# Every second 2 MB load of the experts' weights issued by ScalarE instead of SyncE

## The chip, the cores and the metric

The kernel runs on one core of one Trainium2 chip. The metric is the device time of one execution in microseconds; a time quoted for a kernel is the median of its runs, and the profile is of one execution.

## The reference

A two-layer decoder trunk for 256 tokens of width 1024, all in float32. Layer 0: chunkwise retention (4 heads) and a dense SwiGLU (width 2816). Layer 1: sparse attention with compressed, selected and window branches, and then the part that the change touches, a mixture of 8 SwiGLU experts of width 3584, of which each token uses two:

```python
logits = xf @ w_router
top_v, top_i = lax.top_k(logits, 2)
w = softmax(top_v)
gate = sum(one_hot(top_i, 8) * w[..., None], axis=1)
for e in range(8):
    out = out + gate[:, e:e + 1] * swiglu(xf, w_in[e], w_out[e])   # (256,1024)@(1024,7168), (256,3584)@(3584,1024)
```

Each block ends with a layer norm of `alpha * x + f(x)`. The experts' weights are 352 MB of the 444 MB that the kernel reads.

## The kernel before, in words

The program is a list of steps (`step`), emitted in an order written out by hand; each engine runs its own instructions in exactly that order. A step names the weight units that it reads. The driver at the end of `tile_decoder` goes through the list: it converts units ahead of need (`convert`, L238: ScalarE makes the rounded high part `whi`, VectorE the rest `wlo`; in the experts nothing is converted), emits the step, and releases the units that it has read (`release`, L225). When a whole slot is released, `release` calls `load_next`, which emits the next load of the list into the slot that came free. So a load's place in the program is just behind the last reader of its slot, and the engine that issues it waits there for that reader.

Weights come into SBUF in one list of loads. Those of the layers before the experts are 1 MB each (`z.wide` is None, L208). Those of the experts are 2 MB each, 128 partitions by 16 KB (L204, `Slot` with `wide`): `units_m` (L1212) makes 14 for an expert's `w_in` and 7 for its `w_out`, 21 for each of 8 experts, and they are loaded in the order in which they are read. Eight slots of 2 MB hold them: four in `ring` (shared with the earlier layers), one `more` (opened in `moe_open`, L1357, where attention's memory is free) and three `ext` (opened in `moe_more`, L1364, on the memory of `whi` and `wlo`). All these loads are issued by SyncE, into one queue.

An expert has four stages s = 0 to 3 (two 128-column chunks of width per column group, the last stage one): `w_in(e, s)` multiplies the gathered tokens `xg` with four slots (two in stage 3), 32 tokens in each of three groups; the third group is behind a branch on the expert's token count (more than 64 tokens). ScalarE applies SiLU, VectorE multiplies (L1262, L1263), `h_transpose` (L1271) turns the result with PE and copies it to `hT` with ScalarE and VectorE, and `w_out(e, s)` (L1290, matmuls on L1301) follows one `w_in` later. `scatter` adds the expert's result to `X3`. All 256 tokens fit the first pass here, so `overflow` does no trip.

The first eight loads are emitted before the first expert's steps are through. Counted from 0: loads 0 and 1 among the q projections (released by conversions of the output weights' first units, just ahead of `att_scores(0, 0)`), load 2 in the last steps of attention, load 3 in `moe_open`, ahead of the last conversion, loads 4, 5 and 6 in `moe_more`, ahead of `moe_ln0` (layer norm, whose square root on ScalarE, L311, comes with a load of ScalarE's function table), and load 7 behind the first slot of expert 0 (its ring slot had been free long before). In the layer norm, VectorE's L314 is followed by the reciprocal of that root (L315) and the scaling (L322).

Of the kernel before, what the change touches and what calls it, by code (L numbers as in the profile page):

```python
# [33 lines left out]
NRAW = 8  # L34
# [73 lines left out]
def tile_decoder(ctx, tc, x, ret_w_in, ret_gn_g, ret_w_out, nsa_w_kv, cmp_k_pe, cmp_k_w1, cmp_k_w2,  # L108
                 cmp_v_pe, cmp_v_w1, cmp_v_w2, nsa_w_q, nsa_w_out, ffn_w_in, ffn_w_out,
                 moe_router, moe_w_in, moe_w_out, ln_g, ln_b, tab_c, tab_r, out, wst, stop=None, cap=CAP):  # L110
    nc = tc.nc
# [76 lines left out]
        return r  # L188

    ring = sb.tile([128, NRAW * 2048], F32, name="ring")  # L190
    state = {"at": 0, "free": NRAW, "loaded": 0, "conv": 0, "raw": [], "more": [], "ext": []}

    def load(z):
        n = len(z.raws)
        if z.kind == "more":
            ap = ptile([128, n * 2048], F32, "more", bufs=NMORE, lv=0)
        elif z.kind == "ext":
            ap = side["pool"].tile([128, n * 2048], F32, name="ext", tag="ext", bufs=NEXT)
        else:
            i = (state["at"] + z.room - n) % NRAW  # L200
            state["at"] += z.room
            ap = ring[:, i * 2048:(i + n) * 2048]
        if z.wide is not None:
            nc.sync.dma_start(ap, z.wide() if callable(z.wide) else z.wide)  # L204
        for i, r in enumerate(z.raws):
            r.ap = ap[:, i * 2048:(i + 1) * 2048]
            for view, src in r.parts:
                nc.sync.dma_start(view(r.ap), src)  # L208

    def load_next(kind="raw"):  # L210
        i = state["loaded"]
        if i < len(order) and not (kind != "raw" and order[i].last):
            if kind == "raw":
                n = len(order[i].raws)
                order[i].room = n + state["at"] % n
                if state["free"] < order[i].room:
                    return False
                state["free"] -= order[i].room
            state["loaded"] += 1
            order[i].kind = kind  # L220
            state[kind].append(order[i])
            load(order[i])
            return kind == "raw"
# [185 lines left out]
    def ptile(shape, dt, tag, bufs=1, lv=-1):  # L409
        return phases[lv][1].tile(shape, dt, name=tag, tag=tag, bufs=bufs)  # L410
# [1227 lines left out]
```

## Time and profile before

| | us |
|---|---|
| median of 3 runs (lowest to highest) | 1444.34 (1441.13 to 1444.92) |
| profiled execution: time, span | 1444.41, 1442.5 |
| PE busy | 1354.2 (94%) |
| VectorE (DVE) busy | 471.3 (33%) |
| ScalarE (ACT) busy | 346.8 (24%) |
| DMA, whole span | 450.78 MB, 313 GB/s |

PE is the matrix engine, DVE is VectorE, ACT is ScalarE, SP is SyncE, POOL is GpSimd; a q behind a name (SPq, ACTq) is the engine's sequencer, which waits and issues DMAs without being counted as busy. L204 is line 204 of the kernel. In a timeline row stand the start and the duration in us, the engine, the line, the operation, what is written and read, the shapes and the count of merged instructions, and in brackets the engine's idle time before it with what ended it. The profiled execution is within the runs shown.

### The profile page before, as it was taken

How to read it: one execution, taken by the hardware profiler on the slowest of the kernel's cores; microseconds unless marked ns; L12 is line 12 of the kernel's file. 1: busy time of each engine (PE TensorE's matmuls, PEld its weight loads, DVE VectorE, ACT ScalarE, POOL GpSimd, SP SyncE). 2: the span in 40 equal slices, each digit the busy share in tenths (PEclk: the TensorE clock that was granted, in tenths of full speed). 3: DMA queues.
4: the chain of work that ended last, by engine and by line, in shares of the span. 5: the costliest groups of instructions: out<-in, count | busy, mean ns of one | idle time of the engine just before them, and what ended most of it. 6: DMA issues, size and time to landing. Idle time of an engine off the chain costs nothing. (4 is left out here: it accounts for less than half of the span.)

```text
span 1442.5 us, 25322 instructions
## 1 busy us (share of the span) xinstructions
PE 1354.2 (94%) x11073; PEld 777.8 (54%) x11073; DVE 471.3 (33%) x845; ACT 346.8 (24%) x653; POOL 62.7 (4%) x74
## 2 busy tenths in 40 slices
PE   8999999999999898899999999989999998879995
PEld 7888878999977657534334333333333343223341
DVE  5756776455574886100100100101001101001002
ACT  4433434444544563200100101011001010000002
POOL 3101101000011100200000000000000000000000
PEclk9999999999999999799999999999999999999997
DMA  9736444555444305899999999999999999999960
GB/s 386 270 137 228 152 186 145 198 203 192 176 152 149 144 1 214 330 426 424 426 426 425 426 425 424 426 424 426 426 426 426 426 425 426 425 425 426 425 269 33
DMA packets 39829, 450.78 MB, mean 313 GB/s; under 512 B 4544, under 2 KB 4704, under 8 KB 7952
## 3 DMA queue, kind: packets, MB, share of 16 engines
q1 hardware_dynamic: 38016, 443.76, 75.1%
q0 software_dynamic: 1536, 4.98, 1.0%
q8 instruction: 108, 1.77, 0.5%
q14 instruction: 25, 0.20, 0.0%
q10 hardware_dynamic: 144, 0.07, 0.0%
HBM read 447.74 MB, written 1.05 MB: 311 GB/s over the span
## 5 line engine op out<-in xcount | busy, mean ns | idle before, releaser
L1239 PE MATMUL mm<-ring,xg 128*32 128x512 f32 (+1 forms) x2336 | 235.8, 554 | 9.9 <-DMA ring<-w_moe_a_dram 5.9
L1263 DVE TENSOR_TENSOR msh<-msh,mm 128x256 f32<-128x256 f32 (+1 forms) x96 | 35.4, 386 | 501.2 <-ACT msh L1262 501.2
L248 DVE TENSOR_TENSOR wlo<-ring,whi 128x1024 fp32r<-128x1024 f32 (+2 forms) x162 | 187.7, 1208 | 32.4 <-ACT whi L247 32.1
L1239 PE MATMUL mm<-ext,xg 128*32 128x512 f32 (+1 forms) x1888 | 182.8, 536 | 6.0 <-DMA ext<-w_moe_a_dram 3.0
L1239 PEld LDWEIGHTS mm<-ring,xg 128*32 128x32 f32 x2336 | 77.7, 111 | 157.9 <-issue 133.6
L247 ACT CAST whi<-ring 128x1024 fp32r<-128x1024 f32 (+2 forms) x162 | 153.7, 1008 | 18.9 <-PE acc L257 12.2
L1262 ACT ACTIVATE msh<-mm 128x256 f32<-128x256 f32 (+1 forms) x96 | 32.2, 356 | 485.4 <-PE mm L1239 485.4
L381 PE MATMUL mm<-xTh,whi 128*128 128x256 f32 x448 | 126.7, 283 | 1.6 <-ACT whi L247 1.6
L1239 PEld LDWEIGHTS mm<-ext,xg 128*32 128x32 f32 x1888 | 66.3, 111 | 114.7 <-issue 93.9
L383 PE MATMUL mm<-xTh,wlo 128*128 128x256 f32 x448 | 126.3, 282 | 0.8 <-DVE wlo L248 0.8
L1301 PE MATMUL acc<-ring,hT 128*32 128x512 f32 x1040 | 119.2, 600 | 7.5 <-DMA ring<-w_moe_o_dram 6.5
L382 PE MATMUL mm<-xTl,whi 128*128 128x256 f32 x448 | 126.1, 281 | 0.0
L1301 PE MATMUL acc<-ext,hT 128*32 128x512 f32 x848 | 94.9, 593 | 4.5 <-DMA ext<-w_moe_o_dram 4.2
L381 PEld LDWEIGHTS mm<-xTh,whi 128*128 128x128 f32 x448 | 84.9, 189 | 2.9 <-ACT whi L247 1.9
L383 PEld LDWEIGHTS mm<-xTh,wlo 128*128 128x128 f32 x448 | 85.0, 190 | 1.0 <-DVE wlo L248 1.0
L382 PEld LDWEIGHTS mm<-xTl,whi 128*128 128x128 f32 x448 | 85.0, 190 | 0.8
L1286 DVE COPY hT<-mm 128x256 f32<-128x256 f32 (+1 forms) x32 | 12.4, 389 | 215.7 <-PE mm L1279 215.7
L1301 PEld LDWEIGHTS acc<-ring,hT 128*32 128x32 f32 x1040 | 36.8, 111 | 82.2 <-issue 70.1
L1284 ACT COPY hT<-acc 128x512 f32<-128x512 f32 (+1 forms) x32 | 17.1, 535 | 223.1 <-PE acc L1279 146.9
L1239 PE MATMUL mm<-more,xg 128*32 128x512 f32 (+1 forms) x640 | 63.2, 541 | 3.8 <-DMA more<-w_moe_a_dram 2.5
L1301 PEld LDWEIGHTS acc<-ext,hT 128*32 128x32 f32 x848 | 29.2, 110 | 65.5 <-issue 56.2
L255 PE MATMUL mm<-whi,xTh 128*128 128x512 f32 (+1 forms) x144 | 55.7, 387 | 0.3 <-ACT xTh L260 0.2
(325 smaller groups left out, 1669.7 us busy)
## 6 DMA issues: line engine op xcount, KB each, us to landing
ring<-w_moe_a_dram SPq DMA_DIRECT2D x55, 2048.0 KB, 27.2
ext<-w_moe_a_dram SPq DMA_DIRECT2D x42, 2048.0 KB, 27.7
ring<-w_moe_o_dram SPq DMA_DIRECT2D x29, 2048.0 KB, 27.7
ext<-w_moe_o_dram SPq DMA_DIRECT2D x21, 2048.0 KB, 27.2
more<-w_moe_a_dram SPq DMA_DIRECT2D x15, 2048.0 KB, 28.5
ring<-w_ffn_b_dram SPq DMA_DIRECT2D x22, 1024.0 KB, 5.8
ring<-w_ret_a_dram SPq DMA_DIRECT2D x16, 1024.0 KB, 8.6
more<-w_moe_o_dram SPq DMA_DIRECT2D x6, 2048.0 KB, 26.5
```

Source lines behind the costliest of these rows:

```text
L247: nc.scalar.copy(u.hi, v)
L248: nc.vector.tensor_sub(u.lo, v, u.hi.bitcast(F32))
L255: nc.tensor.matmul(ps, xh, wh, start=start, stop=False, skip_group_check=True)
L381: nc.tensor.matmul(ps, u.hi[:, k], xh[:, k], start=start and k == 0, stop=False, skip_group_check=True)
L382: nc.tensor.matmul(ps, u.hi[:, k], xl[:, k], start=False, stop=False, skip_group_check=True)
L383: nc.tensor.matmul(ps, u.lo[:, k], xh[:, k], start=False, stop=k == KD - 1, skip_group_check=True)
L1239: nc.tensor.matmul(M["A", g][j * 32:(j + 1) * 32, :n], M["xg", e // 2][:, k, e % 2, g * 32:(g + 1) * 32], v[:, kk, j], start=k == 0, stop= ...
L1262: nc.scalar.activation(sh[:, g, :w], M["A", g][:, :w], AF.Silu)
L1263: nc.vector.tensor_mul(sh[:, g, :w], sh[:, g, :w], M["A", g][:, w:2 * w])
L1284: nc.scalar.copy(dst, src)
L1286: nc.vector.tensor_copy(dst, src)
L1301: nc.tensor.matmul(M["y", g][q:q + 32], hT[0][:, g, cc, j * 32:(j + 1) * 32], v[:, c, h], start=s == 0 and i == 0, stop=s == 3 and i == 1, ...
```

## The change

In `load` the engine that issues a 2 MB load alternates: the first, third, ... stay with SyncE, the second, fourth, ... are issued by ScalarE, which has a DMA queue of its own. The 1 MB loads stay with SyncE. Nothing else is moved: slots, order of loads and places of emission are as before.

```diff
-    state = {"at": 0, "free": NRAW, "loaded": 0, "conv": 0, "raw": [], "more": [], "ext": []}
+    state = {"at": 0, "wide": 0, "free": NRAW, "loaded": 0, "conv": 0, "raw": [], "more": [], "ext": []}
...
         if z.wide is not None:
-            nc.sync.dma_start(ap, z.wide() if callable(z.wide) else z.wide)
+            eng = nc.sync if state["wide"] % 2 == 0 else nc.scalar
+            state["wide"] += 1
+            eng.dma_start(ap, z.wide() if callable(z.wide) else z.wide)
```

## Rows read from the trace of the kernel before

**Rows 1.** The page: busy us by engine, and the DMA engines' busy tenths in 40 slices.

```profile
PE 1354.2 (94%) x11073; PEld 777.8 (54%) x11073; DVE 471.3 (33%) x845; ACT 346.8 (24%) x653; POOL 62.7 (4%) x74
...
DMA  9736444555444305899999999999999999999960
```

**Rows 2.** Stretches: length, busy us (instructions) of PE PEld DVE ACT POOL, PEclk, DMA share, GB/s.

```profile
597.00:900.00 303.00, 294.08 (x2873) 111.67 (x2877) 30.74 (x79) 30.20 (x71) 2.92 (x6) 1.00 1.00 423
1160.00:1300.00 140.00, 119.34 (x1152) 44.87 (x1148) 14.18 (x35) 12.87 (x33) 1.97 (x4) 0.98 1.01 425
1300.00:1393.00 93.00, 92.23 (x868) 33.24 (x864) 9.92 (x20) 7.63 (x17) 0.00 (x0) 1.00 0.97 410
1393.00:1421.00 28.00, 28.00 (x319) 11.36 (x311) 2.57 (x6) 2.58 (x6) 0.00 (x0) 1.00 0.14 55
```

**Rows 3.** The loads of L204: an issue's duration ns (min/median/max), and time to landing.

```profile
L204 SPq DMA_DIRECT2D ring<-w_moe_a_dram x55: 327/328/589, 474.9 to 1335.4; - x55
...
DMA to landing us min/median/max: 8.0/27.9/36.8
```

**Rows 4.** Timeline of PE, 1284 to 1302 us: matmuls slot by slot.

```profile
1284.82 3.64 PE L1301 MATMUL acc<-ring,hT 128*32 128x512 f32 x32 [1.52 <-DMA ring<-w_moe_o_dram]
1290.58 5.34 PE L1301 MATMUL acc<-ring,hT 128*32 128x512 f32 x32 [2.12 <-DMA ring<-w_moe_o_dram]
1296.65 5.36 PE L1239 MATMUL mm<-ring,xg 128*32 128x512 f32 x48
1301.79 5.36 PE L1239 MATMUL mm<-more,xg 128*32 128x512 f32 x48
```

**Rows 5.** Timeline around load 1, 479 to 485 us.

```profile
479.55 2.00 ACT L247 CAST whi<-ring 128x1024 fp32r<-128x1024 f32 x2
...
480.64 2.36 DVE L248 TENSOR_TENSOR wlo<-ring,whi 128x1024 fp32r<-128x1024 f32 x2 [1.43 <-ACT whi L247]
...
481.94 0.33 SPq L204 DMA_DIRECT2D ring<-w_moe_a_dram  x1
...
484.24 1.94 DVE L910 TENSOR_REDUCE anm<-mm 128x2 f32<-128x256 f32 x4
...
484.69 0.37 ACT L912 ACTIVATE ae<-mm,anm 128x128 f32<-128x128 f32 x1 [1.84 <-DVE anm L910]
```

**Rows 6.** Timeline of ACT at the start: its one DMA issue.

```profile
0.73 0.40 ACTq L121 DMA_DIRECT2D ident<-tab_c_dram  x1
```

**Rows 7.** Timeline of SP: loads 3 to 7.

```profile
553.49 0.38 SPq L204 DMA_DIRECT2D more<-w_moe_a_dram  x1
569.42 1.28 SPq L204 DMA_DIRECT2D ext<-w_moe_a_dram  x3
570.74 0.59 SPq L204 DMA_DIRECT2D ring<-w_moe_a_dram  x1
```

**Rows 8.** Timeline around loads 4 to 6, 559 to 570 us.

```profile
559.38 1.28 ACT L311 ACT_TABLE_LOAD   x1
...
565.99 0.29 ACT L311 ACTIVATE rs<-mv,epst 128x1 f32<-128x1 f32 x1 [5.32 <-DVE mv L309]
...
568.79 0.15 DVE L315 RECIPROCAL rs<-rs 128x1 f32<-128x1 f32 x1
...
569.00 0.39 PE L257 MATMUL acc<-whi,xTl 128*128 128x512 f32 x1
```

**Rows 9.** Timeline where the first expert starts, 591 to 592 us.

```profile
591.36 1.94 PE L1239 MATMUL mm<-ring,xg 128*32 128x512 f32 x8
591.46 0.48 ACT L1202 COPY xg<-acc 128x384 f32<-128x384 f32 x1 [1.23 <-PE acc L1198]
```

## The prediction, on record before the result was known

> **What bounds the kernel now.** I read the page first, then a table of stretches, then the waits of the experts' stage, then single instructions where ScalarE would have to issue a load. The page says that PE is busy 94% of the span, but the row of DMA slices is full from slice 17 on [rows 1]. The table of stretches separates the two [rows 2]: from 597 us to 1393 us the DMA share is 1.00 to 1.01 at 423 to 425 GB/s (0.97 in the last part, where the loads run out). In 1160:1300 PE is busy only 119.34 of 140 us, so there the loads set the pace; in 1300:1393 and 1393:1421 PE is full and eats what has landed. Of the loads, 168 in all (8 experts by 21 slots), each is 2.097 MB, so one takes 2.097/0.425 = 4.93 us of the 16 engines; the median lands 27.9 us after its issue [rows 3], so 27.9/4.93, between five and six, are under way at a time. The last wait of PE for a load is the one of 2.12 us before 1290.58 [rows 4]: the second slot of `w_out` of expert 6, stage 2, which is load 145 counted from 0. From there to the end PE waits for no load. The end is therefore: when the MoE stage's DMA starts to run without a pause, plus the transfers up to load 145, plus PE's work behind it. SyncE's issue is not in that sum: an issue takes 0.328 us [rows 3] beside 4.93 us of transfer.
>
> **The change, part by part.** Even loads (0, 2, ...) stay with SyncE, odd ones (84) go into ScalarE's instruction stream at the place where the code calls `load`, and ScalarE stands still there until the slot is free.
>
> *Bandwidth.* The bytes are the same and the 16 engines are full [rows 2]: 0. What a second queue could add is rival C.
>
> *Load 1.* SyncE issued it at 481.94, when VectorE had made the low half of a unit [rows 5]. In ScalarE's stream it stands between the two casts of 479.55 (2.00 us for both). So the second cast, which began at about 480.55, now begins after 481.94 plus an issue of 0.40 us (the only issue by ScalarE in the trace [rows 6]), at 482.35, and ends at 483.35. VectorE's second low half, which ran from about 481.85, follows at 483.45: 1.6 us late. VectorE is in order, so the rotary products behind it and the maxima of 484.24 move too, and the exponentials of 484.69 wait for those maxima [rows 5]. The attention that follows is a ring of the three engines with no slack I can see. Cost 1.6; between 0 (something later hides it) and 1.75 (the cast's whole delay).
>
> *Load 3.* It falls between the last split of attention and the last cast. Its memory was free when SyncE issued it at 553.49 [rows 7], so it costs one issue, 0.4 us, and PE still has three earlier units to multiply: 0; 0.4 if that cover is gone.
>
> *Load 5.* It stands behind load 4 in `moe_more`, ahead of the square root of the first layer norm. Its slot lies on the cast weights, which PE reads until 569.00 + 0.39 = 569.4; SyncE's group of three started at 569.42 [rows 7, 8]. ScalarE now stands there. Queued behind it are the table load (1.28 us; done in the shade at 559.38 before) and the square root (0.29, at 565.99), and the reciprocal on VectorE at 568.79 waits for that [rows 8]. New time: 569.4 + 0.4 (issue) + 1.28 + 0.29 = 571.4, 2.6 us after 568.79. Behind the reciprocal VectorE works without a gap until the router, so the experts start 2.6 later. Bounds: 1.3 if the table load stays ahead of the DMA, 3.0 if the two issues also wait for each other, 0.4 us.
>
> *Load 7.* SyncE issued it at 570.74 [rows 7]; ScalarE reaches it behind the gathers' copies, at about 592 [rows 9]. It is the eighth slot to be read, at least 7 by 3.64 us [rows 4] after the experts' start at 591.36 [rows 9], and by then loads 4 to 6 are through (3 by 4.93 us from 570), so it goes alone and lands within some 8.0 us [rows 3]: 0; it would cost its transfer, 4.9, if the next load already stood behind it.
>
> So the unbroken run of transfers starts 1.6 + 2.6 = 4.2 us later. Nothing gives this back, since from there on the engines were already full.
>
> *Issues among the experts.* 80 odd loads at 0.40 are 32 us of an engine that is busy 30.20 of 303 [rows 2]. ScalarE waits there for PE to finish a slot, and what is queued behind (SiLU, the copy of hT) needs PE to be further on still. hT is read one `w_in` later. 0 for PE; the queue of loads is five deep, so an issue 1 us late costs the DMA nothing. Without that cover: 11 odd loads from 147 to 167 by 0.40 = 4.4 us.
>
> *Order of landing.* Now two loads are under way in two queues. If the engines serve both in turn, a load ends after part of its successor has been moved. When the two queues' ends alternate evenly, each load ends half a load, 2.5 us, later than in one line; when they go in step, the first of a pair ends 4.9 later and the second as before. No row shows two such queues at once, so: 0 if they are served one after the other, 4.9 at most. The issue times at the start of the stage are some 4 us apart, alternately, so I take nearly even: 2.5 for load 145. The next slot is read at 1296.65 and landed at about 1290.5 + 4.93 = 1295.4, so it has 1.2 us of slack and does not add. Against it: after the wait of 2.12 the 32 matmuls of 1290.58 took 5.34 against 3.64 us at 1284.82 [rows 4]; at other landing times that slow group may go, which gives back at most those 1.2 us before the next load binds. I take 2.0; ends -1.2 and 4.9. The Trainium skill (DMA: Bandwidth & Descriptors, Queues, rings and completion order) has each DMA engine go round its queues packet by packet; by that rule it is the 2.5, not the 0.
>
> **Sum.** The profiled execution took 1444.41 us for a span of 1442.5, and the median shown is 1444.34, so the sum can be read against either: 1444.41 + 1.6 + 2.6 + 2.0 = 1450.6. With all lower ends 1444.41 + 0 + 1.3 - 1.2 = 1444.5, with all upper ends 1444.41 + 1.75 + 3.0 + 4.9 = 1454.1.
>
> **Rivals.**
> *B, no difference.* ScalarE's stops before the experts are hidden, or the attention makes load 1 good, and only the landing order or one stop remains: 0 to 4 us, 1444.4 to 1448. For it: ScalarE is busy only 24% of the span [rows 1], and of its four loads before the experts two cost nothing by the above. Against it: the reciprocal at 568.79 has VectorE idle for nothing else. That ScalarE's loads do not get a queue of their own ends here too; it issues one transfer in the trace already [rows 6], so I give it little.
>
> *C, faster.* Two queues feed the engines without a small gap between packets, which a share of 1.00 could still hide. Place: the 693 us from 597 to 1290. Price: 1% more rate is 6.9 us. To beat the 4.2 us and then 0.3% it takes 4.2 + 4.3 = 8.5 us, 1.2% or 430 GB/s; no stretch in [rows 2] is above 425 and all say that the engines are full. At 1.5% it would be 1444.41 + 4.2 - 10.4 = 1438. The Trainium skill (same page, Bandwidth) gives 435 GB/s as the fabric's ceiling; by it there are 2.3% to be had at most, and no run here shows more than 425 over a long stretch.
>
> *D, slower still.* ScalarE's issues do come between PE and its inputs in the last stretch, where PE is full: 11 issues, 4.4 us more than the forecast, 1455. It decides from the first issue that PE has to wait for. For it: PE is busy 92.23 of 93 us there, so any wait counts in full. Against it: ScalarE is busy only 7.63 of those 93 [rows 2].
>
> **How the numbers follow.** 0.3% is 4.33 us, about what a measurement of this kernel can tell from no change: faster is below 1440.0, slower above 1448.7. Forecast 0.58, with its own range 1446.5 to 1454; about 0.08 of it lies under 1448.7. B 0.24, C 0.08, with D 0.10. Slower: 0.50 + 0.10 = 0.60. Same: 0.24 + 0.08 = 0.32. Faster: 0.08. The range leaves out C and the lowest part of B below, and the far part of D above: 1443.8 to 1455.5.
>
> **What would show it.** In the profile after: issues by ScalarE, 84, beside 84 by SyncE; the table load before the first layer norm and its square root at about 571.4 and 572.7 instead of 559.4 and 566.0, and the reciprocal's idle time put down to ScalarE; the first expert matmul at about 595.6 instead of 591.4; DMA share still 1.00 at 425 GB/s; landings in pairs or evenly spread, and PE's last wait for a load at about 1297 instead of 1290.6. The forecast is wrong if the first expert matmul starts within 1 us of 591.4 (B), if the rate in 600:1290 rises above 429 GB/s (C), or if PE shows new idle time after its last wait for a load (D).

## The result, and the profile after

The changed kernel took 1453.61 us (median of 5; 1451.27 to 1453.93) against 1444.08 us (median of 5; 1441.13 to 1444.92): 1.0065 times the time, 95% interval 1.0048 to 1.0081, or 9.5 us slower. 1450.6 was predicted: right direction, 3.0 us too little. The experiments below are set against 81 more executions of the kernel before, which took 1440.4 to 1450.1 us, longer ones at a lower mean granted clock (in the first set of 35, 0.001 of clock goes with 0.84 us, correlation -0.89), so each ratio is against executions of its own set. A figure with a plus sign is the ratio less one, times before's median; the ratio is worked out over all executions and need not be that of the two medians.

The page of the kernel after, the lines that answer to [rows 1], and the two queues with packets, MB and share:

```profile
PE 1359.3 (94%) x11073; PEld 783.3 (54%) x11073; DVE 471.5 (32%) x845; ACT 347.5 (24%) x653; POOL 62.7 (4%) x74
...
DMA  9736454555534304799999999999999999999960
...
q1 hardware_dynamic: 25920, 267.60, 45.7%
q10 hardware_dynamic: 12240, 176.23, 28.8%
```

The second queue is there (q10 carries the 84 loads of 2.097 MB = 176 MB), and the engines do the same work. The four stretches that answer to [rows 2], each about 10 us later, with the same columns:

```profile
606.00:909.00 303.00, 292.40 (x2861) 110.28 (x2860) 30.73 (x79) 31.36 (x71) 2.93 (x6) 1.00 1.01 426
1170.00:1310.00 140.00, 118.56 (x1161) 44.87 (x1157) 14.18 (x35) 13.10 (x33) 1.98 (x4) 0.99 1.01 426
1310.00:1403.00 93.00, 92.17 (x864) 31.72 (x860) 9.92 (x20) 7.64 (x17) 0.00 (x0) 1.00 0.97 408
1403.00:1431.00 28.00, 28.00 (x323) 11.42 (x315) 2.38 (x6) 2.58 (x6) 0.00 (x0) 1.00 0.12 47
```

The rate (426 for 423 to 425 GB/s) and PE's share are nearly as before, so the lateness was there when the experts started. The next fences show where it came from. First ScalarE and VectorE at load 1, beside [rows 5]:

```profile
481.77 1.05 ACT L249 CAST whi<-ring 128x1024 fp32r<-128x1024 f32 x1
484.11 0.34 ACTq L206 DMA_DIRECT2D ring<-w_moe_a_dram  x1
484.49 1.04 ACT L249 CAST whi<-ring 128x1024 fp32r<-128x1024 f32 x1 [1.67 <-DVE wlo L250]
...
488.48 0.37 ACT L914 ACTIVATE ae<-mm,anm 128x128 f32<-128x128 f32 x1 [1.65 <-DVE anm L912]
```

```profile
485.57 1.23 DVE L250 TENSOR_TENSOR wlo<-ring,whi 128x1024 fp32r<-128x1024 f32 x1 [1.49 <-ACT whi L249]
486.71 0.42 DVE L713 TENSOR_TENSOR t1k<-acc,C 128x256 f32<-128x256 f32 x1
...
488.04 1.34 DVE L912 TENSOR_REDUCE anm<-mm 128x2 f32<-128x256 f32 x3
```

ScalarE stands 1.67 us between the two casts, as foretold, and VectorE's low half, rotary products and maxima move with the second cast. This execution was already 2.2 us late at 467 us, ahead of every changed load, so that much of its 9.3 us is not the change's; of the 3.8 us at the maxima (488.04 against 484.24) about 1.6 are load 1's. Then PE:

```profile
488.40 1.38 PE L854 MATMUL acc<-ident,qn 128*128 128x128 f32 x4 [2.06 <-POOL qn L719]
...
492.45 6.87 PE L863 MATMUL acc<-kc,qT 128*128 128x30 f32 x32
```

The same two places in the kernel before:

```profile
484.61 0.44 PE L852 MATMUL acc<-ident,qn 128*128 128x128 f32 x2 [0.50 <-POOL qn L717]
...
487.95 3.66 PE L861 MATMUL acc<-kc,qT 128*128 128x30 f32 x32
```

This is what the prediction did not have. PE waits 2.06 us for the rotated queries, where before it waited 0.50, and from then on runs at half its clock: the 32 matmuls of 492.45 took 6.87 us where the kernel before took 3.66. Stretches of after (first four) and before (last four) show the granted clock, the number behind POOL's:

```profile
480.00:490.00 10.00, 7.94 (x53) 5.50 (x52) 7.25 (x11) 5.38 (x13) 1.94 (x3) 0.91 0.89 342
490.00:500.00 10.00, 10.00 (x44) 8.98 (x45) 4.35 (x17) 4.27 (x18) 0.00 (x0) 0.50 0.08 34
500.00:510.00 10.00, 8.58 (x42) 4.92 (x38) 8.86 (x28) 3.92 (x15) 0.00 (x0) 0.73 0.01 2
510.00:520.00 10.00, 8.13 (x51) 5.15 (x52) 7.43 (x23) 5.59 (x23) 0.00 (x0) 0.83 0.01 2
```

```profile
480.00:490.00 10.00, 9.25 (x62) 6.14 (x60) 8.78 (x25) 6.64 (x20) 1.41 (x2) 1.00 0.73 274
490.00:500.00 10.00, 6.32 (x43) 4.48 (x42) 8.37 (x26) 4.99 (x19) 0.00 (x0) 0.96 0.01 2
500.00:510.00 10.00, 9.66 (x58) 5.19 (x57) 7.43 (x26) 5.15 (x20) 0.00 (x0) 0.87 0.00 0
510.00:520.00 10.00, 9.14 (x72) 5.62 (x70) 8.52 (x29) 7.25 (x32) 0.00 (x0) 1.00 0.01 2
```

0.50 is 1.2 GHz instead of 2.4 for the whole ten microseconds. Counting (1 - clock) x 2 x 10 us per row, PE ran 20.6 us at half clock here in after and 3.4 us in before. At 505 us PE of after is 8.4 us late, and VectorE and ScalarE are 8.5 us late from 508 us of before up to load 5.

Load 5, ScalarE and VectorE, beside [rows 7, 8]:

```profile
577.74 0.34 ACTq L206 DMA_DIRECT2D ext<-w_moe_a_dram  x1
578.11 1.28 ACT L313 ACT_TABLE_LOAD   x1 [10.03 <-PE acc L259]
579.40 0.29 ACT L313 ACTIVATE rs<-mv,epst 128x1 f32<-128x1 f32 x1
```

```profile
575.38 1.28 DVE L316 SCALAR_TENSOR_TENSOR msh<-msh,mv,ygb 128x1024 f32<-128x1024 f32 x1 [0.88 <-DMA ygb<-in_ln_g_dram]
579.73 0.16 DVE L317 RECIPROCAL rs<-rs 128x1 f32<-128x1 f32 x1 [3.07 <-ACT rs L313]
```

The table load, done in the shade before, stands behind the load, and the reciprocal waits 3.07 us for ScalarE. The slot came free 8.3 us later than before (577.74 for 569.42); the reciprocal is 10.9 us late (579.73 for 568.79): 2.6 us of load 5's own. Last, PE's waits beside [rows 4]:

```profile
1292.55 5.35 PE L1241 MATMUL mm<-ring,xg 128*32 128x256 f32 x64 [2.65 <-DMA ring<-w_moe_a_dram]
...
1302.19 3.64 PE L1303 MATMUL acc<-ring,hT 128*32 128x512 f32 x32 [0.64 <-DMA ring<-w_moe_o_dram]
```

Load 145 ends PE's last wait at 1302.19, 11.6 us later than before; the span is 9.3 us longer. The 32 matmuls that took 5.34 us at 1290.58 in before take 3.64; the slow group is now the one of 1292.55.

### The profile page after: what moved, and what is told of

Same layout as the page of the kernel before. It is cut to its first block, busy times and chain, and to the rows that moved or that the text cites. A ratio compares the mean times of both kernels' runs of the same rounds, so it can differ in the third digit from the quotient of the medians.

```text
span 1451.8 us, 25301 instructions
## 1 busy us (share of the span) xinstructions
PE 1359.3 (94%) x11073; PEld 783.3 (54%) x11073; DVE 471.5 (32%) x845; ACT 347.5 (24%) x653; POOL 62.7 (4%) x74
```

## The experiments

The theory: ScalarE's stops at loads 1 and 5, the first with the fall of PE's clock behind it. Rivals: the landing order of two queues; a clock fall that was one execution's own. One expression chooses the engine of a load; the kernels below change it or what is shown.

**Load 1 alone, and with a filler.**

```
-            eng = nc.sync if state["wide"] % 2 == 0 else nc.scalar
+            eng = nc.scalar if state["wide"] == 1 else nc.sync
```

> Only load 1 (the second 2 MB load, in the attention stage) is issued by ScalarE; all other loads are SyncE's, so one queue serves the experts. Theory (ScalarE stands still in front of the second cast, TensorE then waits about 2 us for the ropes and its granted clock falls to half in the following stretch): the stop's own net delay +1.5 us and about +4.7 us in the slow stretch, so +4 to +6.5 us in all, 1448 to 1450.5 us beside 1444.1, and the profile shows one wait of TensorE of about 2 us for the rotated queries near 486 us and a granted clock near 0.5 in the ten microseconds after it. Rival A (landing order and two queues make the cost): within 1 us of before. Rival B (the fall of the clock was one execution's own and has nothing to do with the stop): +1.5 us, 1445.6 us, with the clock at 490 to 500 us as before.

1447.80 us; 1.0008 [0.9990, 1.0025] of before (1446.17 us, 35 executions).

The filler kernel has the same edit and, in the transposes of the last rotated queries:

```
+                if i == 3:
+                    for _ in range(12):
+                        nc.tensor.matmul(ps[:, 0:256], identb, maskb.rearrange("p b k -> p (b k)"),
+                                         start=True, stop=True, skip_group_check=True)
```

> As the kernel with load 1 alone on ScalarE, and twelve bf16 matmuls of 128x256, with no use, put on TensorE directly in front of the transposes of the last rotated queries, into the bank that the transposes then overwrite: some 2 us of work where TensorE waited 2.06 us. Theory (TensorE's wait brings the clock down): the granted clock stays near full from 486 to 500 us and the time is 3 to 5 us under that with load 1 alone, 1445 to 1446.5 us. Rival (the clock falls whatever TensorE does there): the clock is near 0.5 again and the time is equal to load 1 alone or up to 2 us above it. Rival (the delay runs through VectorE and ScalarE, not TensorE's rate): clock up, time equal to load 1 alone within 1 us.

1446.26 us; 1.0002 [0.9986, 1.0019]. The traces answer better than the times. In both the clock is at half from 488 or 489 us on (13.6 us at half clock in 480:520): the fall is no accident of one execution. The twelve matmuls took 1.47 us, not 2, and PE still waited:

```profile
483.82 1.47 PE L854 MATMUL acc<-maskb,identb 128*128 128x256 bf16 x12
486.07 0.44 PE L858 MATMUL acc<-ident,qn 128*128 128x128 f32 x2 [0.77 <-POOL qn L719]
486.75 0.44 PE L858 MATMUL acc<-ident,qn 128*128 128x128 f32 x2 [0.24 <-POOL qn L719]
```

So this filler could not decide; one of seventeen follows below. The time of load 1 alone, +1.2 us (-1.4 to +3.6), is at odds with the theory's +4 to +6.5 and fits rival B's +1.5, though B's unchanged clock is not there. Its span is 3.4 us longer than that of [rows 1]'s trace, but it had 13.6 us at half clock in 560:600 where before had 20.4, and before itself stood 2.5 us higher in this set (mean 1445.95 us at clock 0.982) than in the two later ones (1443.44 and 1443.56 at 0.984).

**Load 5 alone.**

```
+            eng = nc.scalar if state["wide"] == 5 else nc.sync
```

> Only load 5 (of the three issued when the first phase's weight buffers come free) is issued by ScalarE. Theory: the activation table's load for the square root waits behind it, the reciprocal of VectorE starts 2.4 us later, and the first expert matmul with it: +2.4 us, 1446.5 us, less what an earlier return of TensorE's clock ahead of the experts gives back (up to 2 us). Rival (two queues alone cost): within 0.5 us of before.

1444.19 us; 0.9992 [0.9974, 1.0011]. The stop is in the trace (issue at 571.15, table load 571.52), and the transposes behind the layer norm are 4.36 us late where the slot was 1.73 us late: 2.6 us again. The time doesn't show it in this set: -1.2 us, at most +1.6, where +2.4 was expected.

**The queues alone.**

```
+            eng = nc.scalar if state["wide"] >= 8 and state["wide"] % 2 == 1 else nc.sync
```

> The first eight loads are SyncE's, and of the later ones every odd one is ScalarE's: neither ScalarE's stop at load 1 nor that at load 5 is left, while from load 9 on two queues share the DMA engines as in the changed kernel. Theory (stops ahead of the experts make most of the cost): +0 to +2 us, 1444 to 1446 us. Rival A (landing order, two queues and ScalarE's issues among the experts make most of it): +6 to +9.5 us, 1450 to 1453.6 us. Rival C (two queues move more bytes a second): under 1443 us.

1446.03 us; 1.0002 [0.9986, 1.0019]: two queues from load 9 on cost nothing that this set can tell (+0.3 us, -2.0 to +2.7). Rival A falls, and nothing speaks for C.

**The changed kernel again, and the early loads by themselves.** The first without an edit.

> The changed kernel once more, with more executions, since the kernel before alone spread from 1441.0 to 1450.1 us over 35 executions and follows its mean granted clock (0.978 near 1449.5, 0.986 near 1441.5). Theory (the change costs what its first five executions showed): 9 us, 1454 to 1455.5 us beside 1446. Rival A (part of the 9.5 us was the clock of five executions each): 4 to 6 us, 1450 to 1452 us. Rival B (mostly scatter): within 2.5 us of before.

```
+            eng = nc.scalar if state["wide"] in (1, 3, 5, 7) else nc.sync
```

> Only loads 1, 3, 5 and 7 are ScalarE's; from load 8 on all are SyncE's. Theory (the four ScalarE loads ahead of and at the start of the experts delay the start, and two queues cost nothing): as the changed kernel, 5 to 9 us over before. Rival (the two queues among the experts cost, but only together with the late start): 2 to 3 us over before, the sum of load 1 alone (+1.3) and load 5 alone (-0.8 to +1), and the changed kernel 3 us or more above it.

```
+            eng = nc.scalar if state["wide"] in (1, 5) else nc.sync
```

> Only loads 1 and 5 are ScalarE's. Theory (the two stops are all): equal within 1.5 us to the kernel with loads 1, 3, 5 and 7 on ScalarE. Rival (the stops hardly count; loads 3 or 7 bring what is left): within 1.5 us of before while that kernel is 4 us or more above it.

Against before's 1441.92 us (29 executions): changed 1453.57 us, 1.0068 [1.0043, 1.0093], +9.8 (6.2 to 13.4); four early loads 1450.32 us, 1.0049 [1.0033, 1.0066], +7.1; loads 1 and 5 1449.72 us, 1.0045 [1.0030, 1.0060], +6.5. The 9.5 us come again, and two loads of 84 carry two thirds. Loads 3 and 7 add 0.6, nothing that shows; the changed kernel is 2.7 above the four early loads, with intervals that overlap.

**Same queues, loads 1 and 5 issued later.** All odd loads are ScalarE's; the counter has gone one up where it is asked, so 2 and 6 are loads 1 and 5. Step 187 comes behind the eight exponentials, step 255 behind the first row's layer norm:

```
+            if state["wide"] in (2, 6):
+                state["late"].append((eng, ap, src))
...
+        if n in (187, 255):
+            while state["late"]:
+                eng, ap, src = state["late"].pop(0)
+                eng.dma_start(ap, src)
```

> All odd loads are ScalarE's as in the changed kernel, but load 1 is issued only behind the eight exponentials that follow the second cast, and load 5 only behind the first row's square root. So the queues are those of the changed kernel and ScalarE stands still at neither place. Theory (the stops ahead of the experts make the cost): the second cast and the table's load start as in before, and the time is within 2 us of before. Rival (two queues make it, whatever ScalarE does): equal to the changed kernel within 1.5 us.

1445.34 us; 1.0016 [0.9997, 1.0034], +2.3: 7.5 us of the 9.8 are gone though 84 loads are still ScalarE's. Place, not engine, made most of the cost. The theory asked for within 2 us, so 2.3 is a little over, with an interval down to -0.4. ScalarE of that kernel at load 5:

```profile
568.12 0.29 ACT L317 ACTIVATE rs<-mv,epst 128x1 f32<-128x1 f32 x1 [5.16 <-DVE mv L315]
569.97 0.33 ACTq L1541 DMA_DIRECT2D ext<-w_moe_a_dram  x1
573.18 1.25 ACT L1084 COPY yhl<-mm 128x512 f32<-128x512 f32 x2 [4.77 <-PE mm L1083]
```

The issue now falls into ScalarE's own wait for PE.

**One of the two moved.** The list of moved loads is cut to one, first to load 1, then to load 5:

```
-            if state["wide"] in (2, 6):
+            if state["wide"] in (2,):
```

> As the changed kernel, but load 1 alone is issued later, behind the eight exponentials; load 5 stays in front of the table's load for the square root. Theory (the time is the landing of load 8 plus a stream of 793 us plus 43 us; load 1's stop with the longer half-clock stretch behind it delays load 8 by 4 to 6 us, load 5's by 2 to 3): +3.5 to +5.5 us over before, some 5 us under the changed kernel, half-clock time between 480 and 520 us back at 3 to 7 us. Rival (the two only cost together): within 2.5 us of before, like the kernel with both moved (+2.3).

```
-            if state["wide"] in (2, 6):
+            if state["wide"] in (6,):
```

> As the changed kernel, but load 5 alone is issued later, behind the first row's square root; load 1 stays between the casts. Theory (terms add): +6 to +7.5 us over before, 2 to 3 us under the changed kernel; half-clock time between 480 and 520 us stays at 13 us or more. Rival (load 1 alone is given back ahead of the experts, as the single look at load 1 alone suggested with +1.3 us): +2 to +4 us over before.

Against before's 1443.15 us (17 executions): load 1 moved 1447.81 us, 1.0034 [1.0021, 1.0047], +4.9; load 5 moved 1451.80 us, 1.0060 [1.0047, 1.0073], +8.7. So load 1 is worth 9.8 - 4.9 = 4.9 us, load 5 between 9.8 - 8.7 = 1.1 and 4.9 - 2.3 = 2.6. The differences are less sure than they look, with intervals of 3.0 to 6.8 us for load 1 moved and 6.8 to 10.5 for load 5 moved: load 1's part is clear (the slowest execution with load 1 moved, 1448.36 us, is under the fastest of the changed kernel's eleven, 1450.78), load 5's by the times is not. The rival that both only cost together falls, and so does the one that load 1's cost is given back ahead of the experts. With load 1 moved the half-clock time in 480:520 is 6.8 us; with load 5 moved it stays at 13.6.

**The gap filled in the changed kernel.** The filler of above with one number changed:

```
-                    for _ in range(12):
+                    for _ in range(17):
```

> The changed kernel with seventeen bf16 matmuls of 128x256, with no use, in front of the transposes of the last rotated queries: 2.1 us by the 0.1225 us of one in the run with twelve, where TensorE waits 2.06 us. Theory (a gap on TensorE brings its clock down): with the wait under 0.4 us the clock stays up until 492 us or later and the time falls by 3 to 5 us against the changed kernel. Rival (what brings it down is the rest of this stretch, not the gap): the clock is at half from 488 to 489 us on as in the changed kernel and in the run with twelve, and the time is that of the changed kernel within 1.5 us.

1450.18 us; 1.0042 [1.0029, 1.0055], +6.1 (4.2 to 7.9): 3.7 us back for work that computes nothing. The two intervals overlap and the sets differ (before's means by 0.1 us), but the slowest of these six executions (1450.68) is under the fastest of the changed kernel's eleven (1450.78). The load is where the change put it, ScalarE stands as long; only PE's gap is closed. PE, and then the stretches of 480 to 520 us:

```profile
485.89 2.02 PE L854 MATMUL acc<-maskb,identb 128*128 128x256 bf16 x17
488.12 0.44 PE L858 MATMUL acc<-ident,qn 128*128 128x128 f32 x2 [0.21 <-POOL qn L719]
...
491.46 4.03 PE L867 MATMUL acc<-kc,qT 128*128 128x30 f32 x32
```

```profile
480.00:490.00 10.00, 9.54 (x69) 6.95 (x68) 7.19 (x13) 5.67 (x14) 1.66 (x3) 1.00 0.89 347
490.00:500.00 10.00, 10.00 (x56) 7.33 (x57) 7.72 (x24) 5.99 (x26) 0.00 (x0) 0.73 0.06 25
500.00:510.00 10.00, 6.67 (x43) 4.01 (x43) 7.49 (x24) 4.37 (x18) 0.00 (x0) 0.93 0.01 2
510.00:520.00 10.00, 9.49 (x67) 5.25 (x63) 8.26 (x33) 6.34 (x27) 0.00 (x0) 1.00 0.00 0
```

The clock is full in 480:490 (0.91 in after), the 32 matmuls that took 6.87 us take 4.03, and the half-clock time is 6.8 us instead of 20.6 (17.2 in the repeat). The clock still falls, at 494 us, but for far less long: the gap makes the long stretch at half clock, and the rival falls.

**Load 7 back on SyncE as well**, on the kernel with loads 1 and 5 moved:

```
-            eng = nc.sync if state["wide"] % 2 == 0 else nc.scalar
+            eng = nc.scalar if state["wide"] % 2 == 1 and state["wide"] != 7 else nc.sync
```

> As the kernel with loads 1 and 5 moved (+2.3 us), and load 7 back on SyncE: there ScalarE issued it at 593.9 us instead of 570.7 behind its copies, it landed at 602.2 instead of 592.7, and load 8, issued 3.7 us after it, took 11.3 us instead of 8.8. Theory (load 8's landing sets the time): load 8 takes about 8.8 us again, and the time is 1 to 2.5 us under that kernel, within 1.5 us of before. Rival (load 7 late costs nothing, since the stream after it is shorter by the same 2 us: 792.3 against 794.2): equal to that kernel within 1 us, the stream near 794 us again.

1445.45 us; 1.0014 [1.0002, 1.0027], +2.0. Load 8 lands 9.5 us after its issue instead of 11.3, and the stream behind it is 1.5 us longer; the time is within 1 us of the kernel with load 7 on ScalarE. The rival holds: load 7's place costs nothing that shows.

## What the traces have in common

Worked out from each trace: time at half clock in two stretches (counted as above), issue and landing of load 8, landing of the last load (167), and the span, all in us.

```
kernel                  half 480:520  560:600   load 8 issue  lands   last lands   span
queues alone                 6.8       17.0        595.0      603.8     1397.5    1440.7
before                       3.4       20.4        596.9      605.7     1399.9    1442.5
load 1 moved                 6.8       17.0        596.6      607.9     1400.3    1443.2
1, 5 moved; 7 SyncE          3.4       17.0        596.6      606.1     1399.9    1444.1
1 and 5 moved                3.4       17.0        597.6      608.9     1401.1    1444.5
load 1 + 12 fillers         13.6       13.6        599.2      607.4     1402.6    1444.5
load 5 alone                 3.4       17.2        598.5      607.6     1401.8    1444.8
load 1 alone                13.6       13.6        599.8      608.7     1403.0    1445.9
loads 1 and 5               17.2       20.4        602.8      611.9     1405.1    1446.3
load 5 moved                13.6       13.8        600.5      611.6     1404.1    1446.8
loads 1, 3, 5, 7            17.0       20.4        603.1      613.2     1406.7    1448.4
changed + 17 fillers         6.8       20.6        601.2      613.7     1404.7    1448.5
changed, again              17.2       20.4        602.6      613.8     1406.2    1449.0
changed                     20.6       19.6        605.5      616.9     1409.2    1451.8
```

From load 8's landing to the last one it is 791.0 to 795.2 us, and from there to the end 41.2 to 44.2 us, in all fourteen; the landing of load 8 moves by 13.1 us and carries the span with it. (One execution each: a span may lie some us off its kernel's median.)

Part of that is the execution's own. Load 0, which SyncE issues ahead of every change, was issued between 474.7 and 477.3 us (474.89 in before, 477.30 in after, 474.74 in the repeat). Reckoned from its issue, the first expert matmul starts after:

```
no stop (before; queues alone; 1 and 5 moved; that with 7 on SyncE)    116.4 to 116.8 us
load 5's stop alone (load 5 alone; load 1 moved)                       117.7, 117.9
load 1's stop alone (load 1 alone; + 12 fillers; load 5 moved)         120.7 to 121.4
both stops (loads 1 and 5; 1, 3, 5, 7; changed; changed, again)        124.0 to 124.4
both stops, PE's gap filled (changed + 17 fillers)                     120.4
```

The groups do not overlap. Load 1's stop costs 4 to 5 us there without load 5's and 6 to 7 with it, load 5's 0.9 to 1.6 us without load 1's and 2.6 to 3.7 behind it, and closing PE's gap gives back 3.6 to 3.9. From load 0's issue to the end it is 967.6 us in before, 974.5 in changed and 974.3 in the repeat: 6.9 and 6.7 us longer, less than the 9.5 and 9.8 of the times.

## Why the prediction was right, and where it was short

*The bound.* Right. After load 8 the engines move bytes without a pause at 423 to 426 GB/s, and what comes late there stays late: from load 8's landing to the end it is 834.4 to 838.0 us in all fourteen traces. Rival C (a higher rate) and rival D (new waits in the last stretch: PE is busy 92.17 of 93 us) did not happen; rival B is excluded by the interval of the repeat. The first expert matmul of after, foretold for 595.6, is at 601.7 (598.8 in the repeat).

But "Nothing gives this back" did not hold. In before PE reads the first expert slot at half clock, in the repeat at full clock:

```profile
591.36 5.34 PE L1239 MATMUL mm<-ring,xg 128*32 128x512 f32 x32
```

```profile
598.78 3.64 PE L1241 MATMUL mm<-ring,xg 128*32 128x512 f32 x32
```

Load 8 is issued when that slot has been read, so 1.7 us of the late start come back there: reckoned from load 0, the first expert matmul is 7.6 us late in the repeat, the issue of load 8 only 5.9.

*Load 1.* The step that failed, a term of the sum that was mis-sized: "Cost 1.6; between 0 ... and 1.75 (the cast's whole delay)". The stop itself measures 1.4 us in the repeat's trace, which has no late start (PE's transposes at 486.05 for 484.61). But I took PE to run at the same speed behind its gap. The gap of 2.06 us put it at half clock over the matmuls that follow; VectorE and ScalarE of the same trace are 5.0 us late from 495 us of before on and 5.6 from 508 on. With the gap filled they are 2.0 us late, less that execution's own late start of 2.1. By the times, moving the load gives back 4.9 us and closing PE's gap alone 3.7, so about 1.2 is the stop and 3.7 the clock. Put in place of 1.6, the 4.9 bring the sum to 1453.9.

*Load 5.* Right as to the stop: 2.6 foretold, and 2.6 in three traces from the freed slot to the reciprocal or what follows it. What it adds to the kernel's time is less sure: 1.1 and 2.6 in the two differences of times, whose intervals reach down past zero, -1.2 (at most 1.6) for load 5 alone, and 0.9 to 3.7 at the first expert matmul of the traces. In "What would show it" the table load and the square root stand at 571.4 and 572.7; by the prediction's own sum (569.4 + 0.4, then 1.28) they should be at 569.8 and 571.1.

*Loads 3 and 7, issues among the experts.* Taken at 0. The four early loads cost 0.6 us more than two of them, well inside the intervals; putting load 7 back changed 0.3 us.

*Landing order.* 2.0 foretold. With both stops gone 2.3 and 2.0 remain, the second with an interval of 0.3 to 3.9; the queues alone gave 0.3, at most 2.7. Landings do alternate as assumed, though not always evenly: from load 155 to load 162 of after 4.69 and 5.11 us apart in turn, 9.80 for a pair, twice the 4.90 of before, and in other stretches of that trace 3.5 and 6.4. In the changed kernel load 8 shares the engines with load 7 and lands 11.4 us after its issue instead of 8.8, but the stream behind it is 1.9 us shorter. From load 8's issue to the end it is 845.6 to 847.5 us in the eight traces with two queues among the experts and 843.5 to 846.3 in the six with one, about 1.3 by the means. So the term's size is not contradicted, and its mechanism (load 145 half a load late) is not shown: load 145 and the end are late by much the same as the start.

*Luck.* That 1450.6 came so near is in part luck. In the two traces of the changed kernel, reckoned from load 0, load 1 made ScalarE and VectorE 5.7 and 6.1 us late where 1.6 was in the sum; the 1.7 us given back were not in it; and behind load 8's issue 0.8 and 0.7 us were added where it had 2.0. The errors largely cancel: the end is 6.7 and 6.9 us late for a foretold 6.2.

*Open.* Load 1 alone measured +1.2 us and load 5 alone -1.2, while both together measured +6.5 in another set. Before ran at a lower clock in the first set, which narrows its ratios, and load 1 alone had less half-clock time ahead of the experts (its trace, reckoned from load 0, is 4.5 us late at the first expert matmul and 3.4 at the end); whether these make up the whole difference was not tried. The times make the change cost 9.5 and 9.8 us, the two traces 6.7 and 6.9 from load 0 on; the rest is not accounted for. Before is at half clock for 3.4 us at 500 us without a gap of 2 us; two of nearly that length stand ahead of it, but it is not shown that they are the reason (the kernel with the queues alone is at half clock for 3.4 us from 492 us on, and its longest wait in the ten microseconds ahead is 0.50 us):

```profile
496.65 0.82 PE L933 MATMUL acc<-ident,ae 128*128 128x128 f32 x4 [1.82 <-DVE ae L923]
499.33 1.08 PE L888 MATMUL acc<-ident,sc 128*120 128x128 f32 x4 [1.86 <-DVE asm L918]
```

## What to carry to other kernels

A DMA issue that must wait for its buffer stops everything behind it on that engine (1.67 us between two casts here, 3.07 us of VectorE's time at the layer norm); an engine with 24% load has room for the issue, not for the wait, so put the issue behind what others need and in front of a wait that the engine has anyway. Cost such a stop by what PE does after the gap, not only by the gap: look at the granted clock of the stretch. Where a DMA stream runs full to the end, read the cost of any change from when that stream starts, and in traces reckon from an instruction ahead of the change, since executions differ before it (by 2.6 us here).

## What the runs showed of the hardware that I had not expected

After a wait of 2.06 us PE ran at half clock for most of the next 15 us; all six traces with a wait of 2.06 to 2.08 us there have 13.6 to 20.6 us at half clock between 480 and 520 us, the six without load 1's stop 3.4 to 6.8. With 0.77 us left of that wait the clock still fell, at 488 us, for 13.6 us; with 0.21 us left it stayed full until 494 us. Executions of the unchanged kernel spread by 9.7 us, most of which goes with the granted clock (0.977 to 0.987). And the useless matmuls paid: 2.02 us of them in PE's gap made the changed kernel 3.7 us faster.
